# Entry of the feed-forward part: weight blocks among the row pairs, pair sums in spare rows, sample's sums behind them

## The chip, the cores and the metric

The kernel runs on one core of one Trainium2 chip. The metric is the device time of one execution in microseconds. The core has a matmul engine (TensorE, PE in the profile; its weight loads are PEld), a vector engine (VectorE, DVE), an activation engine (ScalarE, ACT), a general engine (GpSimd, POOL) and an engine whose queue issues most of the transfers (SyncE, SP). Every engine works through its own queue in order.

## The reference

One inference step of a decoder layer, for a prompt of 1024 rows and a sample of 64 rows, with 1024 columns. The part that matters here is the end of the attention half and the start of the feed-forward half:

```
h = h + concatenate([o_gla, o_mla]) @ w_o
n = rmsnorm(h, g_ffn)
a = n @ ffn_w_gate          # 1024 x 2816
c = n @ ffn_w_up
conv = ffn_conv_b + sum(w[j] * full[:, j:j + T] for j in range(3))   # causal, full = [state, a]
y = (silu(conv) * c) @ ffn_w_down
h = h + y
```

and then a gated per-layer embedding is added. All of it is float32 within the tolerance of a split arithmetic (below).

## The kernel before

**Arithmetic.** Every matmul operand is split into a high part (a cast to fp32r, line 115, on ACT) and a low part (source minus high part, line 116, on DVE or, where the code says so, POOL); `split` does both. A product is three matmuls (lines 139 to 141): high by high, high by low, low by high.

**The feed-forward products.** Tiles 0 to 2 are paired with tiles 3 to 5: the two halves of the 1024 columns and the two halves of the 768 rows make a 2 x 2 block form, which is multiplied by seven products in place of eight (a Strassen-Winograd form). The right operands are x11, x21, x22 and the sums t1 = x12 - x11, t2 = x22 - t1, t3 = t2 - x11, t4 = x21 - t2. The weight operands are g0, g1, u0, u1 (two halves of a block of 128 columns of the gate and the up weights) and the sums s1 = u0 + u1, s2 = s1 - g0, s4 = g1 - s2, s3 = g0 - u0, which `ff_weights` makes on POOL. The remaining tiles 6 and 7 and the sample's 64 rows (320 rows together, `xr`) are multiplied plainly (`rest`). A chunk (`ff_chunk`) is one block of 128 of the 2816 feed-forward columns; 22 chunks follow one another. Within a chunk PE's order is g0 by x11, g1 by x21, s2 by t2, s1 by t1, s4 by x22, s3 by t3, u1 by t4, then the rests; each takes the next PSUM bank from `both`, a cycle of six places over three pools (`pd` with three banks, `pm` with two, `p2` with one; a fourth pool, `p2t`, has two).

**The entry.** When the last units of the output projection are done (`wo_unit`, lines 1432 to 1439; the tiles come in the order 6, 7, 0, 3, 1, 4, 2, 5), each tile is normed (`normed`), stored and scaled in place. Tiles 6 and 7 are turned into `xr` (`turned_rest`). Then `turned_pair` turns each of the three row pairs: 16 transposes into four banks (line 1664), a copy of x11 into the tile's own rows (line 1666, ACT), t1 and t2 on DVE (1667, 1668), t3 on POOL (1672), t4 on DVE, written over x11 (1673), and the splits. Then the sample's product of the last projection chunks, `down_sample` (1445, 1448; bank ps_ds), with its fold into `hs` (1454 to 1456); then `last_sums` splits t3 and t4, whose tiles lie where that product's weights were; then the sample is normed; then `ff_weights(0)` loads, sums and splits the first weight block; then the chunks start. The sample's own rows are turned only within chunk 0 (`turned_rest(NT)`).

**Order.** The queues of the engines are not written by hand. A planner issues the instructions: of those that are ready by its own clock, it takes the one that stands first in the program. So the program's order is a priority, and an instruction can be issued ahead of those before it when its engine would have nothing else. `keep_in_program_order` (first matmul of the sample's product) holds one instruction's place; `issue_after(x)` puts what is inside behind x on x's engine, for instructions of that engine alone.

Of the kernel before, what the change touches and what calls it, by code (L numbers as in the profile page):

```python
# [8 lines left out]
F32 = mybir.dt.float32  # L9
# [35 lines left out]
def step_kernel(ctx: ExitStack, tc: tile.TileContext, A):  # L45
# [1392 lines left out]
        h = hrows(t)[:, cs]  # L1438
        dve.tensor_tensor(h, h, ps, ALU.add)

    def down_sample(parts, bank, f, here=False):

        ps = bank([P, 512], "ps_ds")
        for i, (ss_, (wh, wl)) in enumerate(parts):
            m = pe.matmul(ps, ss_, wh, start=i == 0, stop=False)
            if here and i == 0:
                tc.keep_in_program_order(m)
            pe.matmul(ps, ss_, wl, start=False, stop=i == len(parts) - 1)
        fold_sample(ps, f)

    def fold_sample(ps, f):
        hs = z["hs"][:, f * 512:(f + 1) * 512]
        t_ = fold_tile([R, 512], F32, "fd")
        act.copy(t_, ps[R:2 * R])
        dve.tensor_tensor(hs, hs, t_, ALU.add)
        dve.tensor_tensor(hs, hs, ps[0:R], ALU.add)
# [79 lines left out]
    def wo_units():  # L1536
# [3 lines left out]
        for g in range(3):  # L1540
# [3 lines left out]
            for q, (n, f) in enumerate(quarters):  # L1544
                if g == 0 and q == 0:
                    for ld, x in ((wo_rows, 0), (wo_cols, 0)):
                        for c in grp:
                            ld(c, x)
                    for t in range(NT):
                        sp.dma_start(hrows(t), A["x_prompt"][0, t * P:(t + 1) * P, :])  # L1550
                        if t == 3:
                            for ld, x in ((wo_cols, 1), (wo_rows, 1)):
                                for c in grp:
                                    ld(c, x)
                    sp.dma_start(z["hs"], A["x_sample"].rearrange("b t d -> (b t) d"))
                    yield
                for t in range(4 * n, 4 * n + 4):
                    wo_unit(grp, t, f)
                    if q == 2 and t == 4 and g < 2:
                        for e in range(2):  # L1560
                            down_sample([(oTg[:, c], wow[c, e]) for c in grp], pd, e)
# [63 lines left out]
    def p2(shape, name):  # L1625
        return psT.tile(shape, F32, tag="b", name=name, bufs=1)

    turn = [0]

    def both(shape, name):  # L1630
        turn[0] = (turn[0] + 1) % 6
# [21 lines left out]
        return hrows(t)[:, f * 512:f * 512 + 512].rearrange("p (k n) -> p k n", n=P)  # L1653

    def put(t, nm, src, eng):
        split(*(x[:, :, t * P:(t + 1) * P] for x in xb[nm]), src, eng)

    def turned_pair(t):

        pt = {}  # L1660
        for nm, bank, rows, k0 in (("11", p2t, t, 0), ("12", pd, t + 3, 0), ("22", pd, t + 3, 4), ("21", p2t, t, 4)):
            pt[nm] = bank([P, 4, P], "pt")
            for k in range(4):
                pe.transpose(pt[nm][:, k], hrows(rows)[:, (k0 + k) * P:(k0 + k + 1) * P], ident)
        b11, t1, t2, t3 = quarter(t, 0), quarter(t, 1), quarter(t + 3, 0), quarter(t + 3, 1)
        act.copy(b11, pt["11"])
        dve.tensor_tensor(t1, pt["12"], b11, ALU.subtract)
# [4 lines left out]
        pool.tensor_tensor(t3, t2, b11, ALU.subtract)  # L1672
        dve.tensor_tensor(b11, pt["21"], t2, ALU.subtract)
        put(t, "t2", t2, pool)
        put(t, "t1", t1, dve)

    def last_sums(t):
        put(t, "t3", quarter(t + 3, 1), pool)
        put(t, "t4", quarter(t, 0), dve)

    wgu = {}

# [15 lines left out]
        return hl  # L1698

    def ff_weights(f):  # L1700
        fs = slice(f * P, (f + 1) * P)
        raw, hl = [], wroom()
        for nm in ("ffn_w_gate", "ffn_w_up"):
# [6 lines left out]
        w = wgu[f] = {}  # L1710
        w["g0"] = block(g0, dve, hl)
        w["g1"] = block(g1, dve)
        pool.tensor_tensor(s1, u0, u1, ALU.add)
        pool.tensor_tensor(s2, s1, g0, ALU.subtract)
        w["s2"] = block(s2, dve)
        w["s1"] = block(s1, dve)
        pool.tensor_tensor(g1, g1, s2, ALU.subtract)
        w["s4"] = block(g1, dve)
        pool.tensor_tensor(g0, g0, u0, ALU.subtract)
# [536 lines left out]
```

## Time and profile before

| | us |
|---|---|
| median of 3 runs | 2219.48 (2217.44 to 2220.32) |
| profiled execution | 2221.39 |
| its span | 2219.6 |
| PE busy in it | 2134.6 (96%) |
| DVE / ACT / POOL busy | 1666.6 / 1369.1 / 1227.5 |
| mean granted clock of PE | 0.984 |

The profile's times are microseconds from the start of the span; Lnnn is a line of the kernel. In a timeline a row is: start, duration, engine, line, operation, what is written from what, count, and in brackets the idle time before it and what ended it. Where a row stands for several instructions (x3), its duration is from the first start to the last end. In the table of stretches, each engine's busy time is followed by its number of instructions; then come PE's granted clock (1.00 is full speed), the share of the transfer engines and GB/s. Matmuls overlap: a new one starts before the one ahead has ended, so the step from start to start tells the rate.

### The profile page before, as it was taken

The numbers are of one execution on the slowest core, as the hardware profiler recorded it, in microseconds if no ns is written. First come the engines' busy times: TensorE is split into PE (matmuls) and PEld (weight loads), VectorE is DVE, ScalarE is ACT, GpSimd is POOL, SyncE is SP. The second block draws the span as 40 slices with busy tenths as digits, with TensorE's granted clock in tenths as the row PEclk, the third lists the DMA queues.
The fourth block names the chain that finished last, engine by engine and source line by source line (L and its number), as shares of the span: only waits on it lengthen the run. The fifth ranks groups of instructions, "written<-read, shape, count | busy, mean of one in ns | idle before, by whom it ended". The sixth has DMA issues, their size and how long they took to land.

```text
span 2219.6 us, 38384 instructions
## 1 busy us (share of the span) xinstructions
PE 2134.6 (96%) x13460; PEld 1934.7 (87%) x13460; DVE 1666.6 (75%) x2551; ACT 1369.1 (62%) x3726; POOL 1227.5 (55%) x1330
## 2 busy tenths in 40 slices
PE   7999999999999999999999987999999999999999
PEld 6888978878888888887788876999999999888899
DVE  4775676467788888887888878888888886887642
ACT  5576766777778888887777766433333433534631
POOL 5675668576777777777445557666656562011100
PEclk9899999999999999999999998999999999999999
DMA  5343234412342222221521212322232325778321
GB/s 181 110 141 110 77 117 157 141 54 69 104 120 60 64 73 61 60 56 46 167 80 57 76 66 96 105 92 95 91 100 91 100 87 190 238 222 237 98 72 41
DMA packets 204418, 233.07 MB, mean 105 GB/s; under 512 B 42422, under 2 KB 146339, under 8 KB 204227
## 3 DMA queue, kind: packets, MB, share of 16 engines
q1 hardware_dynamic: 188259, 179.49, 25.8%
q0 software_dynamic: 14736, 46.67, 7.3%
q10 hardware_dynamic: 1232, 4.46, 0.5%
q8 instruction: 108, 1.77, 0.3%
q14 instruction: 83, 0.68, 0.1%
HBM read 188.00 MB, written 42.52 MB: 104 GB/s over the span
## 4 chain that ended last, share of the span: by engine, by line
PE 80%; DVE 7%; ACT 5%; DMA 4%; POOL 2%; issue 2%; SPq 0%; DVEq 0%; POOLq 0%; ACTq 0%
PE ps_gu L140 7%; PE ps_gu L141 7%; PE ps_gu L139 7%; PE ks L139 5%; PE ks L141 5%; PE ks L140 4%; PE ps_dn L141 3%; PE ps_dn L140 3%; PE ps_dn L139 3%; PE cpv L645 2%; PE ctp L522 2%; PE ps_lt L278 2%; PE ps_pj L139 2%; PE ps_pj L140 1%; PE ps_pj L141 1%
## 5 line engine op out<-in xcount | busy, mean ns | idle before, releaser
L560 ACT ACTIVATE csq<-ks 128x256 f32<-128x256 f32 x1040 | 392.2, 400 | 88.1 <-PE ks L141 78.0
L565 DVE TENSOR_REDUCE css<-csq 128x16 f32<-128x1024 f32 (+1 forms) x264 | 315.8, 1197 | 63.0 <-ACT csq L560 61.9
L115 ACT CAST wh<-st 128x512 fp32r<-128x512 f32 x176 | 108.4, 619 | 188.6 <-PE ps_gu L140 166.0
L139 PE MATMUL ks<-mv0h,cTh 128*128 128x320 f32 (+1 forms) x520 | 171.9, 333 | 6.9 <-ACT csq L560 3.0
L139 PE MATMUL ks<-mv1h,cTh 128*128 128x320 f32 (+1 forms) x520 | 170.4, 329 | 7.6 <-ACT sn L562 3.6
L604 POOL TENSOR_TENSOR chl<-craw,chl 128x1024 fp32r<-128x1024 f32 x64 | 141.8, 2216 | 57.9 <-ACT chl L603 57.2
L140 PE MATMUL ks<-mv1l,cTh 128*128 128x320 f32 (+1 forms) x520 | 154.0, 298 | 0.0
L140 PE MATMUL ks<-mv0l,cTh 128*128 128x320 f32 (+1 forms) x520 | 153.0, 296 | 0.0
L141 PE MATMUL ks<-mv0h,cTl 128*128 128x320 f32 (+1 forms) x520 | 148.6, 298 | 0.9 <-DVE cTl L116 0.8
L141 PE MATMUL ks<-mv1h,cTl 128*128 128x320 f32 (+1 forms) x520 | 148.9, 300 | 0.0
L630 POOL TENSOR_TENSOR phl<-sn,phl 128x512 fp32r<-128x512 f32 (+1 forms) x64 | 84.8, 1326 | 108.2 <-ACT phl L629 107.9
L116 DVE TENSOR_TENSOR wl<-st,wh 128x512 fp32r<-128x512 f32 x132 | 119.0, 903 | 28.5 <-ACT wh L115 28.5
L116 POOL TENSOR_TENSOR wl<-st,wh 128x512 fp32r<-128x512 f32 x44 | 69.4, 1580 | 103.5 <-ACT wh L115 98.2
L141 PE MATMUL ps_dn<-o 128*128 128x512 f32 x308 | 120.2, 390 | 0.0
L140 PE MATMUL ps_dn<-o 128*128 128x512 f32 x308 | 120.1, 390 | 0.1
L116 DVE TENSOR_TENSOR cTl<-ctp,cTh 128x512 fp32r<-128x512 f32 (+1 forms) x136 | 90.1, 663 | 39.4 <-ACT cTh L115 38.4
L139 PEld LDWEIGHTS ks<-mv0h,cTh 128*128 128x128 f32 x520 | 99.1, 191 | 20.7 <-ACT sn L562 7.1
L562 ACT COPY sn<-ks 128x64 f32<-128x64 f32 x520 | 116.8, 225 | 0.0
L139 PEld LDWEIGHTS ks<-mv1h,cTh 128*128 128x128 f32 x520 | 99.6, 191 | 19.7 <-ACT sn L562 7.4
L1317 POOL TENSOR_TENSOR pl<-p,ph 128x512 fp32r<-128x512 f32 (+1 forms) x96 | 97.1, 1016 | 31.7 <-DVE ph L1316 21.5
L139 PE MATMUL ps_dn<-o 128*128 128x512 f32 x308 | 112.1, 390 | 0.0
L139 PE MATMUL ps_gu<-xrh,wh 128*128 128x320 f32 x352 | 108.6, 309 | 1.1 <-ACT xrh L115 1.1
(672 smaller groups left out, 7875.3 us busy)
## 6 DMA issues: line engine op xcount, KB each, us to landing
raw<-ds SPq DMA_DIRECT2D x77, 256.0 KB
raw<-ffn_w_down SPq DMA_DIRECT2D x66, 256.0 KB
stage<-w_in SPq DMA_DIRECT2D x48, 256.0 KB
st<-ffn_w_gate SPq DMA_DIRECT2D x44, 256.0 KB
st<-ffn_w_up SPq DMA_DIRECT2D x44, 256.0 KB
wr<-ffn_w_down SPq DMA_DIRECT2D x44, 256.0 KB
ds<-cv SPq DMA_DIRECT2D x21, 512.0 KB
oraw<-doT SPq DMA_DIRECT2D x16, 256.0 KB
```

What stands on the lines that cost most here:

```text
L115: cast = act.copy(hi, src)
L116: res = (lo_eng or dve).tensor_tensor(lo, src, hi.bitcast(F32), ALU.subtract)
L139: pe.matmul(ps, ah, bh, start=first, stop=False)
L140: pe.matmul(ps, ah, bl, start=False, stop=False)
L141: return pe.matmul(ps, al, bh, start=False, stop=last)
L278: pe.matmul(ps, x, w, start=first, stop=last)
L560: act.activation(sq[:, f * 256:f * 256 + 256], ks[:, 0:256], AF.Square)
L562: act.copy(o.sn[:, g0 + i, :], ks[:, 256:320])
L565: dve.tensor_reduce(o.ss[:, g0 + i + 1 - n:g0 + i + 1, :].rearrange("p i h -> p (i h)"), sq2[:, :n].rearrange("p i (h n) -> p (i h) n", n= ...
L604: pool.tensor_tensor(ch[:, c0:c1, 128:256], src, ch[:, c0:c1, 0:128].bitcast(F32), ALU.subtract)
L630: pool.tensor_tensor(phl[:, :nt, 64:128], sb, phl[:, :nt, 0:64].bitcast(F32), ALU.subtract)
L1317: pool.tensor_tensor(pl[:, c0:], p[:, c0:], ph[:, c0:].bitcast(F32), ALU.subtract)
```

## The change

- `turned_pair` uses other banks for pair 1 (`p2`, `pd`, `pm`, `pm`), and the order of its operations changes: x11 is split at once, then t1, t2, x21, t2's split, t4, x22. t4 goes into spare rows (`spare`: the rows of tiles 6 and 7, which have been turned and stored), not over x11. t3 and the split of t1 leave the function.
- t3 is computed on DVE, in `last_sums`; before, it was on POOL, in `turned_pair`. t1's splits come later, in a block of their own behind x21 of pair 2.
- `ff_weights` becomes a generator with three parts (`weight_parts`). For block 0, the loads and the splits of g0 and g1 stand directly behind the sample's product; s1, s2 and their splits behind t1's splits (on POOL after the low half of x11 of pair 2); s4, s3, u1 and u0 where the whole stood, behind the norm of the sample.
- The sample's product and its fold are parted: the two products keep their banks, the folds stand behind the second part of the weights, and their scratch is in tile 7's rows, not in a staging tile.
- The cycle of banks starts at place 3, not 0.
- The pool of weight tiles `fw` is opened earlier.

```
-    turn = [0]
+    turn = [3]
...
+        return ps
...
+    def fold_sample(ps, f, t_=None):
         hs = z["hs"][:, f * 512:(f + 1) * 512]
-        t_ = fold_tile([R, 512], F32, "fd")
+        t_ = fold_tile([R, 512], F32, "fd") if t_ is None else t_
...
+    def spare(t):
+        return quarter(6 + t // 2, t % 2)
...
-        for nm, bank, rows, k0 in (("11", p2t, t, 0), ("12", pd, t + 3, 0), ("22", pd, t + 3, 4), ("21", p2t, t, 4)):
+        banks = (p2, pd, pm, pm) if t == 1 else (p2t, pd, pd, p2t)
+        for nm, bank, rows, k0 in zip(("11", "12", "22", "21"), banks, (t, t + 3, t + 3, t), (0, 0, 4, 4)):
...
         act.copy(b11, pt["11"])
+        z["x11"] = put(t, "11", b11, pool)[1]
         dve.tensor_tensor(t1, pt["12"], b11, ALU.subtract)
         dve.tensor_tensor(t2, pt["22"], t1, ALU.subtract)
+        z["x21"] = put(t, "21", pt["21"], dve)[1]
+        put(t, "t2", t2, pool)
+        dve.tensor_tensor(spare(t), pt["21"], t2, ALU.subtract)
         put(t, "22", pt["22"], dve)
-        put(t, "11", b11, pool)
-        put(t, "21", pt["21"], dve)
-        pool.tensor_tensor(t3, t2, b11, ALU.subtract)
-        dve.tensor_tensor(b11, pt["21"], t2, ALU.subtract)
-        put(t, "t2", t2, pool)
-        put(t, "t1", t1, dve)
 
     def last_sums(t):
+        dve.tensor_tensor(quarter(t + 3, 1), quarter(t + 3, 0), quarter(t, 0), ALU.subtract)
         put(t, "t3", quarter(t + 3, 1), pool)
-        put(t, "t4", quarter(t, 0), dve)
+        put(t, "t4", spare(t), dve)
...
+    def weight_parts(f):
...
         w["g0"] = block(g0, dve, hl)
         w["g1"] = block(g1, dve)
+        yield
         pool.tensor_tensor(s1, u0, u1, ALU.add)
         pool.tensor_tensor(s2, s1, g0, ALU.subtract)
         w["s2"] = block(s2, dve)
         w["s1"] = block(s1, dve)
+        yield
         pool.tensor_tensor(g1, g1, s2, ALU.subtract)
...
-    for f in range(2):
-        down_sample([(z["oTm"][:, c], [w[:, 0, f * 512:f * 512 + 512] for w in w45[c]]) for c in (0, 1)] +
-                    [(z["oTm"][:, c - 4], wow[c, f]) for c in (6, 7)], pm, f, f == 0)
+    dsm = [sample_product([(z["oTm"][:, c], [w[:, 0, f * 512:f * 512 + 512] for w in w45[c]]) for c in (0, 1)] +
+                          [(z["oTm"][:, c - 4], wow[c, f]) for c in (6, 7)], pm, f == 0) for f in range(2)]
...
-    for t in range(3):
-        last_sums(t)
+    fw = opened("fw", side="right")
+    first = weight_parts(0)
+    next(first)
+    with tc.issue_after(z["x21"]):
+        for t in range(3):
+            put(t, "t1", quarter(t, 1), dve)
+    with tc.issue_after(z["x11"]):
+        next(first)
+    with tc.issue_after(z["x21"]):
+        for f in range(2):
+            fold_sample(dsm[f], f, hrows(7)[:R, 512:1024])
+        for t in range(3):
+            last_sums(t)
     normed(NT)
     room["hp"].close()
-    fw, fv = opened("fw", side="right"), opened("fv", side="right")
-    ff_weights(0)
+    fv = opened("fv", side="right")
+    for _ in first:
+        pass
```

More of the change, by code (lines that the diff above doesn't have):

```diff
@@ L1439, in wo_unit, with sample_product @@
         dve.tensor_tensor(h, h, ps, ALU.add)
-    def down_sample(parts, bank, f, here=False):
+    def sample_product(parts, bank, here=False):
         ps = bank([P, 512], "ps_ds")
@@ L1560, in wo_units @@
                         for e in range(2):
-                            down_sample([(oTg[:, c], wow[c, e]) for c in grp], pd, e)
+                            fold_sample(sample_product([(oTg[:, c], wow[c, e]) for c in grp], pd), e)
                     yield
@@ L1655, in put @@
     def put(t, nm, src, eng):
-        split(*(x[:, :, t * P:(t + 1) * P] for x in xb[nm]), src, eng)
+        return split(*(x[:, :, t * P:(t + 1) * P] for x in xb[nm]), src, eng)
+    def spare(t):
+        return quarter(6 + t // 2, t % 2)
     def turned_pair(t):
         pt = {}
-        for nm, bank, rows, k0 in (("11", p2t, t, 0), ("12", pd, t + 3, 0), ("22", pd, t + 3, 4), ("21", p2t, t, 4)):
+        banks = (p2, pd, pm, pm) if t == 1 else (p2t, pd, pd, p2t)
+        for nm, bank, rows, k0 in zip(("11", "12", "22", "21"), banks, (t, t + 3, t + 3, t), (0, 0, 4, 4)):
             pt[nm] = bank([P, 4, P], "pt")
@@ L1700, in ff_weights @@
     def ff_weights(f):
+        for _ in weight_parts(f):
+            pass
+    def weight_parts(f):
         fs = slice(f * P, (f + 1) * P)
```

5 lines of the change are left out of this document (2 added, 3 removed).

## The prediction

> **What bounds the kernel now.** I read the page first, then the busy time by stretches around the entry of the feed-forward part, then the timeline of TensorE (PE), and from there the other engines' timelines and the chain of waits backwards.
>
> ```profile
> span 2219.6 us, 38384 instructions
> PE 2134.6 (96%) x13460; PEld 1934.7 (87%) x13460; DVE 1666.6 (75%) x2551; ACT 1369.1 (62%) x3726; POOL 1227.5 (55%) x1330
> ...
> core 0: us, PE busy (x) PEld busy (x) DVE busy (x) ACT busy (x) POOL busy (x), PEclk, DMA share, GB/s
> 1350.00:1355.00 5.00, 2.78 (x12) 2.28 (x12) 4.97 (x8) 2.84 (x7) 5.00 (x4) 0.58 0.00 0
> 1355.00:1360.00 5.00, 4.15 (x13) 3.23 (x12) 4.32 (x7) 2.93 (x6) 4.82 (x5) 0.50 0.00 0
> 1360.00:1365.00 5.00, 2.76 (x10) 1.87 (x8) 3.56 (x6) 3.89 (x9) 2.69 (x3) 0.89 0.00 0
> 1365.00:1370.00 5.00, 1.65 (x4) 1.12 (x4) 5.00 (x5) 3.81 (x9) 4.91 (x4) 0.79 0.37 92
> 1370.00:1375.00 5.00, 4.59 (x15) 4.59 (x16) 3.25 (x3) 0.13 (x1) 4.84 (x7) 0.53 0.04 13
> 1375.00:1393.60 18.60, 16.99 (x98) 15.69 (x96) 15.67 (x20) 11.07 (x20) 13.45 (x12) 1.00 0.34 100
> 1393.60:2200.00 806.40, 806.31 (x4813) 764.46 (x4814) 615.22 (x815) 323.86 (x581) 309.01 (x307) 1.00 0.40 126
> ```
>
> PE is the bound: 96% busy over the span. From 1393.6 to 2200 it stands for 0.09 us of 806.40, at full clock. So whatever PE gains or loses before 1393.6 goes one to one into the end, if the work behind stays as it is. In the 25 us from 1350 to 1375 PE is busy for 15.93 us only, and much of that at a granted clock near 0.5. VectorE (DVE) and GpSimd (POOL) are the full ones there: 4.97 and 5.00 of 5.00 at 1350.
>
> ```profile
> 1352.14 3.16 PE L1664 MATMUL pt<-ident,h 128*128 128x128 f32 x12 [2.58 <-DVE h L1667]
> 1356.16 1.12 PE L1664 MATMUL pt<-ident,h 128*128 128x128 f32 x4 [0.85 <-ACT h L1666]
> 1356.92 0.78 PE L1445 MATMUL ps_ds<-w45h,oTm 128*128 128x512 f32 x1
> ...
> 1362.37 0.39 PE L1448 MATMUL ps_ds<-wdl,oTm 128*128 128x512 f32 x1
> 1368.35 0.69 PE L139 MATMUL ps_gu<-x11h,wh 128*128 128x384 f32 x1 [5.59 <-ACT wh L115]
> ...
> 1372.18 0.52 PE L140 MATMUL ps_gu<-x11l,wh 128*128 128x384 f32 x1
> 1372.50 0.52 PE L141 MATMUL ps_gu<-x11h,wl 128*128 128x384 f32 x1
> ...
> 1382.78 0.33 PE L139 MATMUL ps_gu<-xt3h,wh 128*128 128x384 f32 x1
> 1382.95 0.33 PE L140 MATMUL ps_gu<-xt3l,wh 128*128 128x384 f32 x1
> ...
> 1391.17 0.56 PE L139 MATMUL ps_gu<-xrh,wh 128*128 128x320 f32 x2 [1.09 <-ACT xrh L115]
> ...
> 1393.62 0.42 PE L140 MATMUL ps_gu<-xrl,wh 128*128 128x320 f32 x1 [0.31 <-DVE xrl L116]
> ```
>
> Read downwards: the last transposes of the row pairs wait for the two engines that empty the banks (2.58 and 0.85 us); the sample's product ps_ds runs from 1356.92 to 1362.76; then PE stands 5.59 us for the cast of the first weight block; then it runs at a step of 0.32 us a matmul (1372.18 to 1372.50) where the later step is 0.17 (1382.78 to 1382.95); two last small waits for the sample's turned rows (1.09, 0.31), and it is saturated.
>
> **The change, part by part.** The banks and the pair sums first.
>
> ```profile
> 1349.67 1.27 POOL L116 TENSOR_TENSOR x11l<-h,x11h 128x512 fp32r<-128x512 f32 x1
> 1350.90 1.73 POOL L1672 TENSOR_TENSOR h<-h,h 128x512 f32<-128x512 f32 x1
> ...
> 1347.74 0.68 DVE L1667 TENSOR_TENSOR h<-pt,h 128x512 f32<-128x512 f32 x1
> 1348.34 0.68 DVE L116 TENSOR_TENSOR x21l<-pt,x21h 128x512 fp32r<-128x512 f32 x1
> ...
> 1349.64 0.42 DVE L722 TENSOR_TENSOR oTm<-po_mla,oTm 64x256 fp32r<-64x256 f32 x1
> ...
> 1353.21 0.68 DVE L1673 TENSOR_TENSOR h<-pt,h 128x512 f32<-128x512 f32 x1
> ```
>
> Now pair 0's fourth sum (L1673, 1353.21) overwrites what POOL's L1672 (1350.90, 1.73 us) still reads, and only then is the transposes' bank free. With the fourth sum in rows of tiles 6 and 7, which were turned and stored long before, it waits for nothing of POOL, and pair 1 has four banks of its own. What is left is DVE: operations out of the banks step by 0.60 us (1347.74 to 1348.34), five a pair. ps_ds takes the banks of pair 1, free after ten of them and the oTm operation: 1347.74 + 10 x 0.60 + 0.42 = 1354.2. So ps_ds begins 2.7 us earlier than 1356.92, and, at its present 5.84 us, ends at 1360.0.
>
> The first weight blocks. Their place in ScalarE's (ACT) queue:
>
> ```profile
> 1360.72 0.58 ACT L1454 COPY fd<-ps_ds 64x512 f32<-64x512 f32 x1 [1.98 <-PE ps_ds L1448]
> 1363.90 0.61 ACT L115 CAST xt3h<-h 128x512 fp32r<-128x512 f32 x1
> ...
> 1367.69 1.12 ACT L115 CAST wh<-st 128x512 fp32r<-128x512 f32 x2
> 1374.87 1.14 ACT L115 CAST wh<-st 128x512 fp32r<-128x512 f32 x2 [6.06 <-POOL st L1714]
> ...
> 1344.35 0.92 SPq L1706 DMA_DIRECT2D st<-ffn_w_up  x2
> ```
>
> The two casts that PE waits for stand behind the sample's fold, the casts of xt3 and xt4 and the sample's squares. After the change g0 and g1 come ahead of these; ACT is busy 2.84 and 2.93 us of each 5 from 1350 to 1360, so 1.12 us of casts fits into the cover. The block's four loads move up with it, but on SP's queue they pass nothing: the last two are issued at 1344.35 already. The fold's scratch in tile 7's spare rows in place of a staging tile costs nothing either; the row is free by then. x11 is complete on POOL at 1349.67 + 5 x 1.27 = 1356.0. The first product can thus follow ps_ds at 1360.2, 8.1 us earlier than 1368.35. Without that cover (casts left behind xt3) only the banks' 2.7 us would be left, 1368.35 - 2.7 = 1365.7.
>
> The clock: from 1368.35 to about 1374.7 (granted clock 0.53 from 1370 to 1375) some 19 matmuls of 0.32 us run 0.15 us too long, 2.8 us. With PE active from 1354.2 on without the 5.59 us hole, I keep 0.5 of it. Before, full speed was back by 1375 after a first matmul at 1368.35. The Trainium skill, "TensorE: Matmul & The Clock Gate", section "Part 1: The HAM clock gate", says that half rate ends after about 3.4 us of sustained activity and returns after an idle window as long; by that the hole is what costs the 2.8, and the sum by it would be 0.5 better. The trace agrees in kind (0.79 and 0.53 behind the hole, 1.00 later), though the way back took some 6 us.
>
> So PE alone would reach the sixth product (s3 by t3, now 1382.78) after five products of 12 x 0.174 us at 1360.2 + 0.5 + 10.4 = 1371.1: 11.7 us earlier. That is the upper bound. What feeds it is next late, and this is where I choose.
>
> ```profile
> 1364.59 4.62 POOL L116 TENSOR_TENSOR xt3l<-h,xt3h 128x512 fp32r<-128x512 f32 x3 [0.80 <-ACT xt3h L115]
> 1369.31 1.14 POOL L1466 TENSOR_SCALAR ss<-ss 64x1 f32<-64x1 f32 x1
> ...
> 1371.35 1.27 POOL L1713 TENSOR_TENSOR st<-st 128x512 f32<-128x512 f32 x1
> 1372.70 2.14 POOL L1714 TENSOR_TENSOR st<-st 128x512 f32<-128x512 f32 x1
> ...
> 1375.18 1.29 POOL L1717 TENSOR_TENSOR st<-st 128x512 f32<-128x512 f32 x1
> ...
> 1365.14 4.62 DVE L116 TENSOR_TENSOR xt4l<-h,xt4h 128x512 fp32r<-128x512 f32 x3
> ...
> 1347.70:1381.60 33.90, 29.44 (x37) 0.75 0.13 38
> ```
>
> POOL: s1 and s2 move ahead: 1356.0 + 1.27 + 2.14 = 1359.4, one more xt2 (1.27), then xt3 as soon as ps_ds frees its room: about 1361.4 + 4.62 = 1366.0, the sample's row scale (1369.31 to 1371.35, 2.04) to 1368.1, s4 to 1369.4. With a cast and a subtraction s4 is ready near 1371.5; PE comes there at 1369.0. That alone costs 2.5 us.
>
> DVE: the last row is its busy time from pair 0 to the last low half of s3, 29.44 of 33.90 us. The change adds the three t3 sums to it (POOL gives up three of 1.73). They read two operands from SBUF. Alone such an operation has the 0.60 step of the others; beside POOL the three of xt4 took 4.62 us, 1.54 each. So the addition is 1.8 to 4.6 us, and DVE's list would be done at 1347.7 + 29.44 + 1.8 = 1378.9 at best if every duration stayed, 1381.7 at worst; now 1381.6. I take 1378.4, since POOL has 5.2 us less to do and its share of the long DVE durations falls with it. The Trainium skill, "GPSIMD Engine Reference", section "1. Specifications", says that POOL shares its SBUF interface with DVE operations of two SBUF inputs. By it every t3 sum pays the long duration: the sum would be 2.8 us worse. The xt3 and xt4 rows, each 1.54 us an operation side by side, agree. The sixth product then begins near 1378.4 instead of 1382.78: 4.4 us gained, not 11.7.
>
> Behind it the waits for the sample's turned rows (1.09 + 0.31) go, since the fold stands earlier: 1.4. The loads of chunk 1's weights wait for staging buffers that s1 and s2 free, and move forward with these. The waits of issue_after add nothing of their own: t1's low halves wait behind x21 of pair 2, and the first reader of t1 is the fourth product. The bank turn, shifted by three, costs nothing I can find: a chunk takes nine banks in a cycle of six, so odd and even chunks swap what they have now; bounds 0.5 us either way.
>
> Sum: -4.4 - 1.4 = -5.8 us, between -13.1 (PE's own arrival) and -0.9 (DVE full, each t3 sum long: 1381.7 for 1381.6, less 1.0 of the last waits). The profiled execution took 2221.39 us, its span 2219.6 and 1.8 around it; the median shown is 2219.48, 1.9 lower. I carry the difference over: 2215.6 for such a profiled execution, 2213.7 for the median.
>
> **The rivals.** *DVE is the bound and gives it all back.* For it: 4.97, 4.32 and 5.00 of 5 busy, and moving work there from POOL. Against it: 4.46 us of its 33.90 are idle. Price: the lower bound, -0.9 to -3, some 2217.5. The Trainium skill, "GPSIMD Engine Reference", section "1. Specifications", points to this case as well.
>
> *The split is not moved.* The order is written by a planner that takes the first ready instruction by program order; if it finds no room on ACT or DVE among the pairs, the first product comes at 1365.7 and 2.7 us are gained: 2216.8. Against it: ACT's idle 2 us of each 5.
>
> *Slower: ACT stands in front of s2.* Its queue is in order, and the 6.06 us row shows it standing for POOL's s2. After the change the cast of s2 comes ahead of the fold copies and the xt3 casts. If POOL gets to s2 where I put it (1359.4), nobody waits. From 1366 on (1360.2 + 5.8) the gain is gone. If s2 keeps its present end of 1374.84, fold, xt3 (4.62), row scale (2.04) and s4 (1.29) follow it, with four short ACT and DVE steps of 0.6: 1385.2 for s4 against 1380.70 now, and the weight loads behind. That is +4.5 to +6, about 2225. Against it: s1 and s2 are placed directly behind x11, whose row ends by 1356.0 in my sum.
>
> ```profile
> 1380.70 0.33 PE L139 MATMUL ps_gu<-x22h,wh 128*128 128x384 f32 x1
> ```
>
> (the row of s4's first product now).
>
> **How the numbers follow.** 0.2% is 4.4 us, about what a measurement of this kernel can tell from no change. Forecast with all its variants beyond that, from -4.5 to -13: 0.63. DVE bound 0.18 and split not moved 0.08, both within 0.2%: 0.26. Slower: 0.11. The range leaves out the slower case and the best end of PE's own arrival (beyond -11.5, some 0.07): 2208.0 to 2219.5. The forecast's own range is 2208 to 2215.
>
> **What would show it.** In the changed profile: no L1672 on POOL; ps_ds from about 1354; the first ps_gu right behind it, with no wait of 5 us for wh; the sixth product (xt3h) near 1378, and the waits before it, on wl or xt3l, naming DVE or POOL; no wait over 0.3 us from about 1388. Wrong would be: a first product later than 1366, a wait of ACT for L1714 of several us ahead of the fold, or new PE waits within the chunks (a wait from 1393.6 to 2200 beyond today's 0.09 us).

## The result: slower by a third of a per cent

The changed kernel takes 2224.84 us in the median (2223.34 to 2231.47 over nine runs), the kernel before 2218.24 beside it (2217.30 to 2221.53). The ratio is 1.0032, its 95% interval 1.0021 to 1.0042: slower by 4.7 to 9.3 us, where 2213.7 had been predicted and the range ended at 2219.5.

The profiled execution of the changed kernel is its longest, 2231.47 us, and 4.0 us of that are lost between 1300 and 1330, ahead of the change and in the same instructions (granted clock 0.74 from 1298 to 1324, where before had 0.93). So all its times below stand about 4.0 later than those of before. To compare executions without such differences I use one number, the **entry**: how much further behind the kernel before TensorE's matmuls stand after the entry (median of those between 1460 and 1500) than ahead of it (1325 to 1335), each matmul paired with the same one of before by tile, shape and order. For the changed kernel that is 10.05 - 3.98 = **+6.1 us**; from there to 2150 the shift stays at 10.05 to 10.06. So the loss arises between 1335 and 1460 and nothing is given or taken later. "On the scale of before" means: less the shift ahead of the entry. The n-th product matmul is the n-th of those that write ps_gu.

The stretches of the changed kernel, each 4.0 later than the prediction's, with one more ahead of them (columns as there; the first row is the same stretch of before):

```profile
core 0: us, PE busy (x) PEld busy (x) DVE busy (x) ACT busy (x) POOL busy (x), PEclk, DMA share, GB/s
1340.00:1350.00 10.00, 7.13 (x57) 5.31 (x57) 9.28 (x14) 9.42 (x20) 8.16 (x8) 1.00 0.63 211
...
1344.00:1354.00 10.00, 7.27 (x51) 5.91 (x49) 8.23 (x10) 8.38 (x18) 7.73 (x7) 0.83 0.63 209
...
1354.00:1359.00 5.00, 2.61 (x12) 2.27 (x12) 4.94 (x7) 2.81 (x6) 2.53 (x2) 0.76 0.00 0
1359.00:1364.00 5.00, 3.65 (x17) 2.68 (x17) 5.00 (x9) 4.53 (x9) 4.12 (x4) 0.90 0.00 0
1364.00:1369.00 5.00, 4.81 (x25) 4.14 (x24) 5.00 (x4) 1.14 (x2) 4.92 (x5) 1.00 0.00 0
1369.00:1374.00 5.00, 1.84 (x7) 1.54 (x8) 5.00 (x7) 2.30 (x5) 2.98 (x2) 0.97 0.00 0
1374.00:1379.00 5.00, 4.17 (x13) 3.51 (x12) 5.00 (x5) 2.61 (x6) 4.83 (x3) 0.50 0.20 55
1379.00:1397.60 18.60, 14.81 (x60) 13.15 (x58) 15.17 (x21) 9.30 (x18) 9.32 (x11) 0.68 0.29 84
1397.60:2204.00 806.40, 804.96 (x4785) 762.10 (x4786) 622.03 (x819) 326.07 (x585) 313.38 (x309) 1.00 0.40 126
```

TensorE does get the block it had stood for: 4.81 of 5.00 at full clock at 1364, where before it had been 2.76 at 1360. Then it falls back: 1.84, then half clock, then 14.81 of 18.60 at 0.68, where before had 16.99 at full clock. Over the last seven rows it is idle 13.2 us (before, the same seven: 10.8), and busy time times the missing share of the clock makes 7.9 us (before 6.1). That is 2.4 + 1.8 of the 6.1. Ahead of 1354 the clock is 0.83 already, which for 7.27 us busy makes 1.2 more; the remaining 0.7 these rows don't place. Nearly all of the loss is there when the first chunk's product with t4 begins: 1390.7 on the scale of before, where before begins it at 1384.9.

TensorE's timeline, with what ended each wait:

```profile
1347.85 0.24 PE L675 MATMUL pt_ol<-ident,late 64*128 64x64 f32 x1 [1.48 <-DVE late L671]
...
1356.39 2.67 PE L1668 MATMUL pt<-ident,h 128*128 128x128 f32 x12 [3.29 <-DVE h L1672]
...
1361.96 0.44 PE L139 MATMUL ps_gu<-x21h,wh 128*128 128x384 f32 x1 [0.68 <-ACT x21h L115]
1364.87 0.39 PE L1445 MATMUL ps_ds<-w45h,oTm 128*128 128x512 f32 x1
...
1372.16 0.50 PE L1445 MATMUL ps_ds<-w45h,oTm 128*128 128x512 f32 x1 [3.35 <-DVE x22l L116]
...
1376.15 0.69 PE L141 MATMUL ps_gu<-xt2h,wl 128*128 128x384 f32 x1 [0.82 <-DVE wl L116]
...
1388.59 0.69 PE L141 MATMUL ps_gu<-x22h,wl 128*128 128x384 f32 x1 [2.63 <-DVE wl L116]
...
1400.36 0.56 PE L139 MATMUL ps_gu<-xrh,wh 128*128 128x320 f32 x2 [0.48 <-ACT xrh L115]
...
1403.92 0.41 PE L140 MATMUL ps_gu<-xrl,wh 128*128 128x320 f32 x1 [0.78 <-DVE xrl L116]
```

The 5.59 us for the weight's cast are gone, and the first product comes at 1361.96, 1358.0 on the scale of before and 10.4 us earlier. In their place stand waits for VectorE: for pair 0's t1 (3.29), for x22l of pair 1, whose bank ps_ds needs (3.35), and for the low half of the fifth weight block s4 (2.63).

VectorE and the two engines that feed it, in that order:

```profile
1353.15 2.58 DVE L1474 SCALAR_TENSOR_TENSOR h<-h,rs,gb 128x1024 f32<-128x1024 f32 x1 [1.77 <-DMA dhp<-h]
1355.65 0.68 DVE L1672 TENSOR_TENSOR h<-pt,h 128x512 f32<-128x512 f32 x1
...
1364.00 3.54 DVE L116 TENSOR_TENSOR xt1l<-h,xt1h 128x512 fp32r<-128x512 f32 x2
1367.46 3.44 DVE L1680 TENSOR_TENSOR h<-h,h 128x512 f32<-128x512 f32 x2
...
1371.43 0.68 DVE L116 TENSOR_TENSOR x22l<-pt,x22h 128x512 fp32r<-128x512 f32 x1
...
1386.65 1.27 DVE L1474 SCALAR_TENSOR_TENSOR hs<-hs,rs,gb 64x1024 f32<-64x1024 f32 x1 [3.22 <-DMA dhs<-hs]
1387.86 1.28 DVE L116 TENSOR_TENSOR wl<-st,wh 128x512 fp32r<-128x512 f32 x2
```

```profile
1343.03 0.59 ACT L1670 COPY h<-pt 128x512 f32<-128x512 f32 x1 [0.24 <-PE pt L1668]
...
1348.33 0.33 ACTq L1592 DMA_DIRECT2D dhp<-h  x1
...
1367.02 1.14 ACT L115 CAST wh<-st 128x512 fp32r<-128x512 f32 x2 [3.47 <-POOL st L1722]
...
1383.53 0.63 ACT L1465 ACTIVATE junk<-hs 64x512 bf16<-64x512 f32 x1 [2.05 <-DVE hs L1456]
...
1384.16 2.16 ACT L115 CAST wh<-st 128x512 fp32r<-128x512 f32 x4
...
1367.07 1.62 POOL L1726 TENSOR_TENSOR st<-st 128x512 f32<-128x512 f32 x1
1368.65 1.71 POOL L1728 TENSOR_TENSOR st<-st 128x512 f32<-128x512 f32 x1
```

Three things are to be seen. Pair 1's x11 is turned and copied (L1670, 1343.03) while tiles are still being normed; the last tile's store is issued at 1348.33, and its norm in place (L1474) waits 1.77 us for that store and runs 2.58 us: the first t1 of the pairs stands at 1355.65, 1351.7 on the scale of before, 3.9 late. Then VectorE's queue has xt1l and the t3 sums (L1680), 1.7 us each beside a busy GpSimd, ahead of x22l at 1371.43. And s4 and s3 (L1726, L1728) are ready at 1370.4, but their casts stand on ScalarE behind the sample's squares, at 1384.16, and their low halves on VectorE behind the sample's norm, which waits 3.22 us for the sample's store.

VectorE's total, from 1340 on the scale of before to the start of the 260th product matmul, of before and then of the changed kernel:

```profile
1340.00:1418.60 78.60, 65.02 (x360) 58.88 (x361) 68.06 (x92) 45.52 (x89) 60.25 (x53) 0.89 0.32 94
```

```profile
1344.00:1428.70 84.70, 68.89 (x359) 61.80 (x358) 77.60 (x95) 44.51 (x88) 57.95 (x49) 0.86 0.29 87
```

VectorE is busy 9.5 us longer with three operations more.

### The profile page after: what moved, and what is told of

Its sections match the earlier page's. It is cut to its first block, busy times and chain, and to the rows that moved or that the text cites. A ratio compares the mean times of both kernels' runs of the same rounds, so it can differ in the third digit from the quotient of the medians.

```text
span 2229.7 us, 38382 instructions
## 1 busy us (share of the span) xinstructions
PE 2141.5 (96%) x13460; PEld 1939.6 (87%) x13460; DVE 1676.4 (75%) x2554; ACT 1370.2 (61%) x3726; POOL 1224.8 (55%) x1327
## 3 DMA queue, kind: packets, MB, share of 16 engines
q8 instruction: 108, 1.77, 0.3%
## 4 chain that ended last, share of the span: by engine, by line
PE 79%; DVE 8%; ACT 6%; DMA 3%; issue 2%; POOL 2%; SPq 0%; DVEq 0%; ACTq 0%; POOLq 0%
PE ps_gu L140 7%; PE ps_gu L141 7%; PE ps_gu L139 7%; PE ks L139 5%; PE ks L141 4%; PE ks L140 4%; PE ps_dn L141 3%; PE ps_dn L140 3%; PE ps_dn L139 3%; PE cpv L645 2%; PE ctp L522 2%; PE ps_lt L278 2%; PE ps_pj L139 2%; PE ps_pj L140 1%; PE ps_pj L141 1%
## 5 line engine op out<-in xcount | busy, mean ns | idle before, releaser
L140 PE MATMUL ps_gu<-xrl,wh 128*128 128x320 f32 x352 | 108.6, 309 | 0.8 <-DVE xrl L116 0.8
```

The source lines that it names most:

```text
L140: pe.matmul(ps, ah, bl, start=False, stop=False)
```

## The experiments

Where single times scatter by some 10 us, three rounds resolve 0.15 of a per cent at best; so each version is judged by its entry too, by the start of ps_ds, and by the 120th and 260th product matmul, all on the scale of before. An entry comes from one execution. Ahead of the change, between 1310 and 1325, the same instructions already lose from 0 to 1.6 us against before from trace to trace (3.0 in the changed kernel), so an entry under some 1.6 us is not told from nothing by itself. The expectations name entries as they were first read, up to 0.4 us from those here (+5.9 for the changed kernel's +6.1, +5.5 for +5.3 of banks_alone).

| version | median us (before beside it) | ratio, 95% | entry us | ps_ds | 120th | 260th |
|---|---|---|---|---|---|---|
| before | | | 0 | 1356.9 | 1395.5 | 1418.6 |
| changed | 2224.84 (2218.24) | 1.0032, 1.0021 to 1.0042 | +6.1 | 1360.9 | 1401.2 | 1424.7 |
| banks_alone | 2224.11 (2220.02) | 1.0014, 1.0000 to 1.0028 | +5.3 | 1361.2 | 1399.9 | 1424.0 |
| sums_alone | 2221.30 (2220.02) | 1.0009, 0.9994 to 1.0024 | +1.9 | 1355.7 | 1397.4 | 1420.5 |
| split_alone | 2220.99 (2220.02) | 1.0003, 0.9986 to 1.0020 | -0.1 | 1360.3 | 1391.0 | 1418.6 |
| after_late_bank | 2224.96 (2220.02) | 1.0021, 1.0005 to 1.0036 | +4.5 | 1366.0 | 1399.6 | 1423.1 |
| banks_alone_held | 2226.32 (2221.26) | 1.0013, 0.9999 to 1.0026 | +6.1 | 1362.3 | 1400.4 | 1424.7 |
| after_held | 2226.91 (2221.26) | 1.0024, 1.0008 to 1.0041 | +6.0 | 1369.4 | 1401.1 | 1424.7 |
| after_sample_last | 2230.10 (2221.26) | 1.0031, 1.0015 to 1.0046 | +7.4 | 1362.4 | 1401.0 | 1426.0 |
| after_old_banks | 2223.60 (2221.26) | 1.0014, 0.9996 to 1.0031 | +4.7 | 1356.6 | 1393.8 | 1423.4 |
| before_relieved | 2220.21 (2220.98) | 1.0003, 0.9990 to 1.0016 | -0.4 | 1356.9 | 1395.0 | 1418.2 |
| split_relieved | 2220.59 (2220.98) | 0.9992, 0.9980 to 1.0004 | -1.5 | 1360.3 | 1392.1 | 1417.1 |
| after_no_t3_sums | 2224.90 (2220.98) | 1.0017, 1.0006 to 1.0028 | +4.7 | 1362.4 | 1399.9 | 1423.3 |
| after_t3_on_pool | 2224.32 (2220.98) | 1.0016, 1.0006 to 1.0026 | +5.9 | 1362.4 | 1401.1 | 1424.6 |
| banks_early_only | 2226.28 (2219.35) | 1.0025, 1.0013 to 1.0037 | +5.7 | 1361.6 | 1400.1 | 1424.4 |
| banks_shared_only | 2225.57 (2219.35) | 1.0024, 1.0011 to 1.0037 | +5.0 | 1360.6 | 1399.5 | 1423.6 |
| old_banks_relieved | 2218.92 (2219.35) | 1.0000, 0.9987 to 1.0013 | +0.9 | 1356.7 | 1394.7 | 1419.5 |
| turn_alone | 2219.87 (2219.35) | 1.0000, 0.9985 to 1.0015 | +0.9 | 1356.9 | 1395.4 | 1419.5 |
| split_relieved_three | 2220.36 (2222.05) | 0.9995, 0.9986 to 1.0004 | -1.6 | 1360.3 | 1392.1 | 1417.0 |
| split_relieved_all | 2216.43 (2222.05) | 0.9982, 0.9972 to 0.9992 | -1.8 | 1360.3 | 1392.2 | 1416.9 |

In the expectations from the second group on: theory A is that pair 1's early turn delays the last norms and is the loss; B, that the pairs collide on VectorE beside GpSimd whenever they begin; C, that the sample's chain stands ahead of s4 and s3; D, that VectorE's list up to about 1415 is a second gate; E, that ps_ds waits for the bank it shares with pair 1. Those of the first group state their theories themselves.

### First group: which part of the change

banks_alone is the kernel before with nothing but the banks and the first turn (its second change in short):

```
-    turn = [0]
+    turn = [3]
-  p2t, pd, pd, p2t                    (11, 12, 22, 21, for every pair)
+  (p2, pd, pm, pm) if t == 1 else (p2t, pd, pd, p2t)
```

> The kernel before with one part of the change alone: pair 1 in the banks p2, pd, pm, pm, and the cycle of banks begun at place 3. Theory: with a bank of its own, pair 1's copy, cast and low half of x11 are issued ahead of the last tiles' norms on ScalarE and GpSimd, the in-place scaling on VectorE then meets the tile's store, and the pairs begin 3 to 5 us late: 2221 to 2223.5 us, with the first t1 on VectorE at 1351 or later (before: 1347.74). Rival (the loss is all VectorE's new load, the banks are harmless): 2216 to 2218.5 us, first t1 at 1347 to 1348.

sums_alone is before with t4 in the spare rows and the t3 sums on VectorE in `last_sums`:

```
-        pool.tensor_tensor(t3, t2, b11, ALU.subtract)
-        dve.tensor_tensor(b11, pt["21"], t2, ALU.subtract)
+        dve.tensor_tensor(spare(t), pt["21"], t2, ALU.subtract)
...
     def last_sums(t):
+        dve.tensor_tensor(quarter(t + 3, 1), quarter(t + 3, 0), quarter(t, 0), ALU.subtract)
         put(t, "t3", quarter(t + 3, 1), pool)
-        put(t, "t4", quarter(t, 0), dve)
+        put(t, "t4", spare(t), dve)
```

> The kernel before with one part alone: the fourth sum in spare rows, the third on VectorE in last_sums; banks and weights as before. Theory: a small effect, -2 to +2 us (2216 to 2220), because GpSimd has no weight sums beside VectorE's third sums there. Rival (VectorE's load is the whole loss): +5 us or more, 2223 or later.

split_alone is before with `weight_parts`, two parts of it ahead of `last_sums`, and the fold's scratch in tile 7's rows:

```
+    fw = opened("fw", side="right")
+    first = weight_parts(0)
+    next(first)
+    next(first)
     for t in range(3):
         last_sums(t)
```

> The kernel before with the weight block's first two parts ahead of the last sums alone, and the fold's scratch in tile 7's rows; banks, pair sums as before. Theory: the first product comes some 4 us earlier, the weight sums on GpSimd lengthen VectorE's operations from SBUF, net -4 to +1 us (2214 to 2219). Rival (s4 and s3 left behind the sample's norm cost as much as is gained, so the split is the loss): 2221 or later.

after_late_bank is the changed kernel with the banks of pairs 1 and 2 exchanged (`t == 2` for `t == 1`), so that the pair with its own banks is the last.

> The changed kernel with the banks of pairs 1 and 2 exchanged: pair 2 takes p2, pd, pm, pm and pair 1 takes p2t, pd, pd, p2t, so that pair 1's first copy cannot be early. Theory: the norms keep their place, the pairs begin as before (first t1 on VectorE within 0.5 us of before, when the ends of the projection are laid on each other), and 3 to 5 us of the 6.6 come back: 2220 to 2222. Rival (banks harmless): 2224 to 2226.

By the traces the banks alone bring +5.3 us where the whole change brings +6.1; the sums +1.9; the split nothing by its end, although its 120th matmul comes 4.5 us early. By the times, none of the three is clear of before (the interval of banks_alone begins at 1.0000). With the banks exchanged the pairs start nearly on time (1348.4), but ps_ds then waits 2.4 us for pair 2, and 4.5 us remain, where the theory had 3 to 5 us coming back. TensorE's waits of banks_alone (us in total, times, longest):

```profile
PE ps_gu L139 <- ACT wh L115: 5.5, 1, 5.5
PE ps_ds L1445 <- DVE x22l L116: 4.1, 1, 4.1
```

The 5.6 us of before are still there, and 4.1 have come ahead of them.

### Second group: the early turn, or what follows it

banks_alone_held and after_held queue the pairs' turns behind the projection's last product (`chain`) and the last tile's last square (`sq`):

```
     for t in range(3):
-        turned_pair(t)
+        with tc.issue_after(z["chain"]), tc.issue_after(z["sq"]):
+            turned_pair(t)
```

> The kernel before with the new banks and first turn alone (as in banks_alone), and the turns of the pairs queued behind the projection's last product on TensorE and behind the last tile's second square on ScalarE: the early turn of pair 1 is taken out of the stretch in which the last tiles are normed, the banks stay. Theory A (the early turn delays the last two norms, and that is the loss): the first t1 is back at 1347.5 to 1348.5 on the scale of before (banks_alone 1351.7), the last in-place norm takes 1.3 us instead of 2.8, and the entry costs between -1 and +1.5 us against before, where banks_alone cost +5.5. Theory B (the banks make the pairs collide on VectorE and GpSimd, whenever they begin): the first t1 is back, but the first product of the sample's sums still starts after 1360 and the entry still costs +3.5 or more.

> The changed kernel with the turns of the pairs queued behind the projection's last product on TensorE and behind the last tile's second square on ScalarE; all else as changed. Theory A: first t1 at 1347.5 to 1348.5 on the scale of before, first product of the blocks about 3.5 us earlier than in the changed kernel (1354.5), entry cost from +5.9 down to between 0 and +2.5. Theory B (queue order on VectorE beside a busy GpSimd): as in after_late_bank, the start is restored and the entry still costs +3.5 to +5. Theory C (the sample's norm in front of the blocks s4 and s3): the wait for the sample's store stays about 3 us, and the product with t4 still starts after 1388.

after_sample_last moves `normed(NT)` behind the weight blocks (gain, sums and scratch in a pool `nm` of their own):

```
-    normed(NT)
     room["hp"].close()
     fv = opened("fv", side="right")
     for _ in first:
         pass
+    normed(NT)
+    room["nm"].close()
```

> The changed kernel with the sample's norm moved in the program behind the casts of the last four weight blocks (its gain, sums and scratch get a pool of their own, so that the residual's room can close first); banks and order of the pairs stay. Theory C: the product with t4 waits no more for its weight (3.5 us of waits go), the entry costs +1.5 to +3 instead of +5.9. Theory A: the pairs still begin at about 1351.7 and ps_ds still waits; at most the waits of the last two products go, and the entry costs +4 to +5.5.

after_old_banks is the changed kernel with `banks = (p2t, pd, pd, p2t)` for all pairs.

> The changed kernel with the banks of before for all three pairs (the first turn of the product's banks stays at the new value); split weights, spare rows, the sums on VectorE and the sample's order stay. Theory A: first t1 at 1347.5 to 1348.5, ps_ds no longer waits for x22 (its bank is free), first product of the blocks at 1354 to 1357, entry -3 to +1 against before. Theory B: the pairs still run into VectorE's list beside GpSimd, entry +2 to +4. Theory C: +2 to +4 with the wait for the sample's store near 3 us.

Theory A fell. Held back, the pairs start at 1349.4 instead of 1351.7 (1.6 later than before still, where 1347.5 to 1348.5 was expected), and the entry is +6.1 and +6.0, where A had at most +1.5 and +2.5: the waits behind them grow. In banks_alone_held, which meets B's mark (+3.5 or more):

```profile
PE ps_ds L1445 <- DVE x22l L116: 7.6, 1, 7.6
```

C fell as well. In after_sample_last the product with t4 comes 4.1 us earlier (1386.6 for 1390.7), and the time is lost behind it: the entry is +7.4 where C had +1.5 to +3. The waits are now others:

```profile
PE ps_gu L139 <- ACT v L1789: 3.3, 1, 3.3
PE ps_gu L139 <- DVE hs L1456: 2.2, 1, 2.2
PE ps_ds L1763 <- DVE ssm L1837: 1.7, 1, 1.7
```

With the old banks ps_ds is back at 1356.6 and the 120th matmul at 1393.8, 1.7 us ahead of before. That part of the entry is thus the banks' doing and the rest of the change gains. But the 260th comes 4.7 us late, so that of the changed kernel's entry only 1.3 us are gone. No theory had put these two together. The place of the loss is the sample's row product of the first chunk, within the second:

```profile
1413.55 0.79 PE L1761 MATMUL ps_ds<-wdh,ssm 128*128 128x512 f32 x1 [3.77 <-DVE ssm L1835]
```

### Third group: a second gate on VectorE

The relief takes work of the first chunk (f == 0) off VectorE that ScalarE can do; in short, and for the sample's rows likewise:

```
-            dve.tensor_scalar(cv[:, n0:n1], a[:, n0:n1], w3[0], w3[3], ALU.mult, ALU.add)
+            act.activation(cv[:, n0:n1], a[:, n0:n1], AF.Identity, scale=w3[0], bias=w3[3])
```

> The kernel before with the first taps of the first chunk's convolution (128x384, 128x640 and 128x64, 2 to 4 us of VectorE between 1385 and 1410) done on ScalarE; nothing of the change. Theory D (from the projection's end to about 1418 VectorE's list, its work beside a busy GpSimd plus its own waits, is what lasts longest once the first products come earlier): before does not feel it, since its TensorE has no wait for VectorE after 1395 and is full from 1400 on; entry -0.7 to +0.7. Rival (VectorE decides in before as well): entry -1.5 to -3.

> split_alone with the same first taps on ScalarE. In split_alone the 200th product of the blocks comes 4.5 us ahead of before (1403.3 against 1407.8) and the 260th no earlier (1418.6), with a wait of 2.8 us for VectorE's last use of the fourth bank and a clock of 0.91 between 1400 and 1420. Theory D: with 2 to 4 us less on VectorE that wait falls below 1 us and the entry gains 2 to 4 us against before (split_alone -0.1). Rival (the second chunk's weights, whose loads land at 1388, are the gate): the wait moves to the weight's low parts and the entry stays within 1 us of before.

after_no_t3_sums leaves out line 1680 and lets `put(t, "t3", ...)` read t2, so part of its output is not the reference's; after_t3_on_pool gives line 1680 to GpSimd.

> The changed kernel without the three sums t3 on any engine (the blocks' seventh product takes t2 in their place, so that this part of the output is not the reference's). On VectorE they took 3.5 + 1.7 us in the changed kernel. Theory D: VectorE's time up to the 260th product falls by 3 to 5 us and the entry from +5.9 to +1.5 to +3.5. Theory A (pair 1's early turn is the loss): they stand behind the late start anyway, entry +5 to +6.

> The changed kernel with the three sums t3 back on GpSimd, in the same place of the program. Theory D: VectorE loses three instructions, but GpSimd's list grows by 3 x 1.7 us that slow VectorE's neighbours; entry +3 to +5. If GpSimd is the bound, the t3 and t4 products come later and the entry is +6 or more.

The kernel before does not feel the relief (-0.4); split_alone does, though less than I expected (-1.5 for -2 to -4): its wait for VectorE's cv, first row, is gone, and in split_relieved a shorter one for ssm, second row, comes next.

```profile
PE ps_gu L139 <- DVE cv L1827: 2.8, 1, 2.8
```

```profile
PE ps_ds L1758 <- DVE ssm L1838: 1.1, 1, 1.1
```

The t3 sums on VectorE were not the cause that I had taken them for: without them +4.7 remains, and on GpSimd +5.9. Both expectations missed. (The three sums took 3.44 + 1.18 us in the changed kernel, not the 3.5 + 1.7 of the expectation.) My reading, which no version tested by itself, is that in the changed kernel TensorE gets to the chunk's tail late anyway, so that work taken from VectorE ahead of it only makes other waits longer.

### Fourth group: the two halves of the banks

banks_early_only has `(p2, pd, pd, p2t)` for pair 1, banks_shared_only `(p2t, pd, pm, pm)`, both with `turn = [3]`; turn_alone has that turn only; old_banks_relieved is after_old_banks with the relief.

> The kernel before with the turn of the product's banks at its new value and, of the new banks, only the first: pair 1's x11 is turned through the bank p2 (early, as in banks_alone), its other three through the old ones, so the sample's bank stays free. Theory E (the loss of the new banks is ps_ds waiting for pair 1 to give its bank back): ps_ds begins at 1356.5 to 1358.5 and the entry costs -1 to +1.5. Rival (the early turn of pair 1 and the late norms): first t1 near 1351.5, ps_ds at 1360 or later, entry +3.5 to +5.5.

> The kernel before with the turn at its new value and, of the new banks, only the other two: pair 1's x22 and x21 are turned in the sample's bank, its x11 through the old bank, so nothing of pair 1 is early. Theory E: first t1 at 1347.7 as before, ps_ds at 1360.5 or later behind pair 1's x22l, entry +3.5 to +5.5. Rival (early turn): entry -1 to +1.

> after_old_banks with the first chunk's first taps on ScalarE. There the 200th product came 1.8 us ahead of before and the 260th 4.8 us behind, with a wait of 3.8 us for VectorE's ssm. Theory D (VectorE's list at 1405 to 1415 is the second gate): that wait falls by 1.5 to 3 us and the entry from +4.9 to +1 to +3.5. Rival (the gate is elsewhere): the entry stays above +4.

> The kernel before with nothing changed but the first turn of the product's banks (3 for 0). Theory E and D: nothing in the entry's waits depends on it, entry -0.7 to +0.7. Rival (the turn changes which bank the second chunk waits for): +1 to +4, with a new wait between 1395 and 1420.

Each half costs about as much as the two together: +5.7 and +5.0, where E had the first half free (-1 to +1.5). By the times too each is slower than before (1.0025 and 1.0024, intervals clear of 1). They do it in different ways. TensorE's timeline of banks_early_only, then of banks_shared_only:

```profile
1353.22 2.31 PE L1664 MATMUL pt<-ident,h 128*128 128x128 f32 x8 [2.86 <-DVE h L1667]
1359.82 2.54 PE L1664 MATMUL pt<-ident,h 128*128 128x128 f32 x10 [4.29 <-DVE x22l L116]
```

```profile
1361.76 0.79 PE L1445 MATMUL ps_ds<-w45h,oTm 128*128 128x512 f32 x1 [6.40 <-DVE x22l L116]
```

With the early half the pairs begin late (first t1 1351.7) and the last turn waits for a bank; with the shared half they begin at 1349.1, and ps_ds itself waits 6.40 us for pair 1's x22l. Either way ps_ds begins at 1360.6 to 1361.6, 3.7 to 4.7 us late, and in these two versions all products stand behind it. That is why holding the early turn back could not help banks_alone: the shared half was left.

Theory D held: in old_banks_relieved the entry falls from +4.7 to +0.9 (expected +1 to +3.5), and the wait for ssm from 3.77 to

```profile
1407.15 0.50 PE L1761 MATMUL ps_ds<-wdh,ssm 128*128 128x512 f32 x1 [1.52 <-DVE ssm L1841]
```

Its time is no longer told from before (1.0000, 0.9987 to 1.0013) and lies clear of the changed kernel's by the intervals. The turn alone has +0.9 in its trace, with a new wait for ssm of 0.7, and what is left of old_banks_relieved is about that; its time (1.0000) shows nothing of it, and so small an entry can be chance.

### A version ahead of both

split_relieved with the first taps of three, and of all, chunks on ScalarE, and with the second chunk's `sample_rows` one product later.

> split_relieved with the first taps of the first three chunks on ScalarE, and the second chunk's first product with the sample's rows one block product later. Theory D: the wait for ssm (1.1 us) and part of the clock lost behind it go as well, entry -2 to -3.5 against before, ratio 0.9985 to 0.9993. If the second gate has moved to the weights of the second chunk (loads landing at 1385), the entry stays at -1.7.

> The same with the first taps of all chunks on ScalarE. TensorE is full from about 1420 on, so that theory D expects no more than in the three-chunk version: the same entry within 0.5 us, and the same time behind it within 1 us. If VectorE still held TensorE somewhere in the later chunks, the shift at 2100 would be lower than at 1480.

The version with all chunks relieved takes 2216.43 us beside 2222.05 of before, 0.9982 (0.9972 to 0.9992), so it is ahead of before and, by the intervals, of the changed kernel. Its trace shows an entry of -1.8 and no gain in the chunks behind it (shift -5.43 at 1480 and at 2100). The version with three has -1.6, short of the -2 to -3.5 expected, and its interval contains 1. So the relieved split gains some 1.5 to 1.8 us by three traces that agree; why the median of one version is 4 us lower than that of the other, the traces don't tell. The wait for ssm was not removed (1.4 us in both).

## Why the prediction was wrong, point by point

- **PE is the bound; what it loses before 1394 goes into the end.** Held: the shift stays at 10.05 to 10.06 from 1480 to 2150.
- **The banks: ps_ds from 1354.2, 2.7 us earlier.** This step failed, and it is the first of two that decide (the second is VectorE's list, below). ps_ds begins at 1360.9, 4.0 later than before. I had counted ten bank operations of 0.60 us on VectorE from an unchanged start. The start moved 3.9 us, because the free bank let pair 1 in among the last norms, and in VectorE's queue xt1l, the t3 sums and weight halves came ahead of x22l of pair 1. I had also named the shared bank (ps_ds takes the banks of pair 1) and not asked what it cost if they came free late. banks_alone shows the price of it by itself, +5.3. The gain had rested on a misread row besides: in the kernel before the L1673 at 1353.21 starts 0.60 us behind the row ahead of it, with no wait; of the three only one waits for GpSimd, 0.56 us, and the transposes' wait of 2.58 us ends with an L1667. sums_alone, with the fourth sum in the spare rows and the old banks, has ps_ds 1.2 us early, at 1355.7.
- **The first product right behind ps_ds at 1360.2, 8.1 us earlier.** Held and exceeded: 1358.0, ahead of ps_ds. The split did what the code says. Being early was not worth what I took it for: split_alone has its 120th matmul 4.5 us early and its 260th at the same time as before.
- **The clock: 2.8 us down to 0.5.** Failed. The hole of 5.59 us became several of 0.7 to 3.4, and half clock came back with each of the longer ones; by the stretches 7.9 us are lost to it where it had been 6.1.
- **POOL: s4 at 1369.4, behind the sample's row scale.** The sum was done by 1364.7, earlier than I had it. What I left out was the queue of ScalarE: the cast stood behind the sample's squares, at 1380.2. after_sample_last showed that this is not the cause by itself.
- **VectorE: 1.8 to 4.6 us for the t3 sums, list done at 1378.4.** The three took 4.6, the upper end. The Trainium skill, "GPSIMD Engine Reference", section "1. Specifications", has GpSimd share its SBUF interfaces with VectorE operations of two SBUF inputs; the trace agrees, 1.57 us each here for the 0.60 step of an operation alone (in the same trace the three xt4l, from 1380.17, take 1.88 us in all while GpSimd stands). The sixth product began at 1381.4 in place of 1378.4, and broke off after two matmuls for the low half of s4. But my list ended at the low half of s3. VectorE's backlog reaches to 1412 and beyond, and I had not looked for what it does to the second chunk. That is the rival "VectorE is the bound and gives it all back", right in kind, for a place that I had not searched: with the old banks it takes 6.5 us between the 120th and the 260th matmul, and with VectorE relieved as well the entry is down to +0.9.
- **The waits for the turned rows, -1.4.** Failed: 0.48 + 0.78 in place of 1.09 + 0.31.
- **The turn of the banks, 0.5 either way.** The trace has +0.9, too little to be told from the 0.5.
- **The slower rival** (ScalarE stands for s2, about 2225) gave the right time for another reason. ScalarE waits 3.47 us for s2 at 1367, but no product waits for that block longer than 0.82 us, and s4's first product, for which the rival had 1385.2, comes at 1380.8, as before (1380.7).

What stays open: the price of VectorE's order among the pairs by itself, since no version changed that alone; the relief in the changed kernel with its new banks, which was not tried, so that the two causes are parted from one side only; and the new banks for other tenants than ps_ds, with ps_ds in a bank that nobody else uses, which was not tried.

## What to carry to other kernels

A bank that is free earlier changes who is issued first, and a planner by readiness will then put early work in front of the work that the path needs; so cost a bank change by the last tenant of each bank, not by the first. And ahead of costing a step that comes earlier, follow the other engines to the point where their backlog ends, not only to the step: here 4.5 us gained at the 120th matmul were gone by the 260th, and moving some 2.5 us of VectorE's work to a less busy engine kept 1.5 of them.

## What the hardware showed that I had not expected

The granted clock is set by stretches of 3.41 us, not by single waits. In all 20 traces it changes only on a grid of that step, which lies differently in each execution. Here are the changed kernel's stretches on its grid (columns as above; the clock is the third number from the end):

```profile
1366.85:1370.26 3.41, 1.96 (x12) 1.64 (x10) 3.41 (x3) 1.14 (x2) 3.33 (x3) 1.00 0.00 0
1370.26:1373.67 3.41, 1.51 (x7) 1.25 (x8) 3.41 (x6) 1.97 (x4) 1.53 (x2) 1.00 0.00 0
1373.67:1377.08 3.41, 2.58 (x8) 1.88 (x7) 3.41 (x3) 2.94 (x6) 3.18 (x3) 0.50 0.00 0
1377.08:1380.50 3.42, 2.74 (x10) 2.27 (x8) 3.31 (x5) 0.22 (x1) 1.83 (x2) 0.50 0.70 214
1380.50:1383.91 3.41, 3.41 (x11) 3.41 (x12) 2.83 (x5) 1.36 (x4) 0.00 (x0) 0.50 0.05 18
1383.91:1387.32 3.41, 1.56 (x7) 0.69 (x5) 0.67 (x1) 3.38 (x9) 1.05 (x4) 1.00 0.35 77
1387.32:1390.73 3.41, 2.14 (x7) 2.15 (x8) 3.41 (x5) 1.44 (x4) 2.74 (x4) 0.50 0.23 66
1390.73:1394.15 3.42, 3.42 (x12) 3.42 (x11) 3.42 (x6) 0.62 (x1) 2.08 (x2) 0.50 0.32 93
1394.15:1397.56 3.41, 3.41 (x25) 3.09 (x24) 3.41 (x4) 2.24 (x3) 3.41 (x3) 1.00 0.19 70
```

TensorE stands 3.35 us up to 1372.16, across two stretches; ps_ds then runs at full step for 1.5 us, and half clock comes with the next stretch, at 1373.67. The waits of 0.82 and 0.68 us leave the next two stretches busy for 2.58 and 2.74 us, and full clock comes back only behind a stretch without a wait, at 1383.91. Over the 20 traces the 268 falls to half clock all follow a stretch that was busy for at most 78%, and the 268 returns one that was busy for at least 86%; a full stretch did not always suffice. So the 0.82 and 0.68 us cost more than their length: they kept half clock on. The Trainium skill, "TensorE: Matmul & The Clock Gate", section "Part 1: The HAM clock gate", gives an idle window of about 3.4 us for the way down and a busy one for the way back. The trace agrees with the way back (1380.50 to 1383.91); the way down came here behind stretches that were still busy for 1.51 and 1.56 us.

A norm in place waits for the store of the same rows. L1474 stood 1.77 us for a tile's store and 3.22 us for the sample's, in a queue where the next operations needed neither; in the kernel before it had waited for the row scale.
